# The down block product of a streaming encoder layer: accumulators first on VectorE, three plain feature pairs instead of two

## The chip, the cores and the metric

The kernel runs on one core of a Trainium2 chip. The metric is the device time of one execution in microseconds (us). One core has a matrix engine (TensorE, PE in the profile; PEld is its weight loading), VectorE (DVE), ScalarE (ACT), GpSimd (POOL) and SyncE (SP), which here only issues DMAs. TensorE accumulates in PSUM; everything else lies in SBUF or in DRAM.

## The reference

One inference step of an encoder layer for 1024 prompt frames and 32 sample frames, in fp32. The part that matters here is the feed-forward block, which stands before and after a token mixer (attention and gated linear attention, which the change doesn't touch):

```python
def swiglu(h, w_gate, w_up, w_down):
    return (jax.nn.silu(h @ w_gate) * (h @ w_up)) @ w_down

x = x + 0.5 * swiglu(rmsnorm(x, g_ffn1), w1g, w1u, w1d)     # FFN1
...                                                         # token mixer
x = x + 0.5 * swiglu(rmsnorm(x, g_ffn2), w2g, w2u, w2d)     # FFN2
x = rmsnorm(x, g_final)
```

The model width is 1024, the hidden width 2816, so `w_down` is 2816 x 1024. Prompt and sample frames share the weights and are treated as 1056 columns.

## The kernel before, in words

Activations are feature-major: `S.x` is eight tiles of 128 features x 1056 frames, the residual. A fp32 product is made of three fp32r products: each operand is split into a rounded high part (ACT, line 51) and the rest (DVE, line 55, or POOL, line 53), and hi·hi, hi·lo and lo·hi are summed in PSUM (`mm3`, lines 60 to 62).

Gate/up and down use one level of the Strassen-Winograd scheme: seven products of blocks for a 2 x 2 block product, in the order 1, 6, 7, 5, 2, 4, 3. Their right-hand sides are the hidden block B11, B21, B22 and the sums T1 to T4. The hidden features are 22 tiles of 128, in 11 pairs; one pair (256 features) is one gate and one up step. For the pairs 1 to 9 the gate/up stage computes the seven right-hand sides of the down product at once, splits them and stores them to DRAM (`keep`, lines 397 to 403: seven parts of 528 KB a pair). The pairs 0 and 10 are stored as plain hidden features (`hid_spill`, line 388 for pair 10; pair 0 is made elsewhere), since 11 is odd and the down stage multiplies two pairs at a time.

The down stage (class `Down`) walks over groups of pairs, `PAIRS = [(1, 2), (3, 4), (5, 6), (7, 8), (9,)]`, and in each group over m = 0..3, that is 256 of the 1024 output features: 20 steps (class `DownStep`). A step has seven products of 12 matmuls (128 x 264 columns), 84 in all; in the last group, which has one pair, 6 each, 42 in all. The seven products accumulate into four PSUM tiles (`pd_a` to `pd_d`, two banks each, one rotating pool of four): 1 and 2 into a, 6 into b, 7 and 4 into c, 5 and 3 into d. So product 3 can start only when what was read from d after product 5 has been read, and product 4 when c has been read after product 7.

What comes out of PSUM (`emit`, lines 498 to 539): `c1` = half of product 1 (ACT, line 523); `half` is one DVE instruction, 0.5·PSUM + y (line 505). It makes `u2` from b and c1, `u3` from c and u2, and adds a, c, d into the four half tiles of x that the step owns. POOL adds `u3` into x11 (line 530), `u2` into x10 (line 533) and `u2` into x01 (line 536). Before the change these POOL additions stand ahead of the DVE addition into the same x (for x11 in the same product's turn, for the others one or two products earlier), so the DVE instruction that reads d after product 5 needs POOL's line 530 done first.

A step's weights are loaded as one slab of 512 KB two steps ahead, and prepared one step ahead (`prep`, called after product 6): four POOL sums (lines 484 to 487), then splits into the weight tiles. Parts of the next group are loaded during a group into the 28 half-tile places of `S.h` and `S.X`. During the last group the hidden features of the plain pairs are loaded (line 630, halves of 264 KB, through the slab buffers) and split, and so are the plain slabs of `w_down`.

Then `plain` multiplies the four plain feature tiles: 3 chunks of 352 columns x 8 output tiles x 4 features x 3 matmuls = 288 matmuls; DVE adds each sum into x (line 654). What follows (a norm and the next projection, or the closing norm) starts out of `plain`.

The order of all instructions on an engine is set at build time by a scheduler that goes by priorities (roughly the order of the code) and models when operands are ready; at run time each engine runs its queue in order and waits on semaphores.

Of the kernel before, what the change touches and what calls it, by code (L numbers as in the profile page):

```python
# [8 lines left out]
F32 = mybir.dt.float32  # L9
# [6 lines left out]
P = 128  # L16
# [257 lines left out]
class Step:  # L274
# [89 lines left out]
    def out(self, q, u, ps):  # L364
# [12 lines left out]
        else:  # L377
# [4 lines left out]
            else:  # L382
                t = two(S.tmp.tile([P, HALF], F32, name="tc", tag="tc"))
                nc.vector.tensor_add(t, u, ps)  # L384
                nc.gpsimd.tensor_mul(two(hid), t, sg)  # L385
            if self.i == FT // 2 - 1:
                f, h = 2 + q // 2, q % 2
                nc.sync.dma_start(S.hidden[f][:, h * HALF : h * HALF + HALF], hid)
            elif q != 1:
                self.keep({0: "B11", 3: "B22", 2: "B21"}[q], hid)  # L390
            else:
                b11, b12, b21, b22 = (S.x[4 + n][:, :HALF] for n in range(4))
                for name, o, x, y in (("T1", b11, b12, b11), ("T3", b12, b22, b12), ("T2", b22, b22, b11), ("T4", b21, b21, b22)):
                    nc.vector.tensor_sub(o, x, y)  # L394
                    self.keep(name, o)
# [68 lines left out]

PAIRS = [(1, 2), (3, 4), (5, 6), (7, 8), (9,)]
PLAIN = (0, 1, 20, 21)


class DownStep:


    def __init__(self, D, g, m):
        self.D, self.S, self.g, self.m, self.n = D, D.S, g, m, len(PAIRS[g])
        self.odd = (4 * g + m) % 2

    def prep(self, raw):

        S, nc = self.S, self.S.nc
        w = self.n * P
        a = [raw[:, i * w : i * w + w] for i in range(4)]  # L480
        s12 = S.s32.tile([P, 512], F32, name="s12", tag="s1")[:, : 2 * w]
        s34 = S.s32.tile([P, 512], F32, name="s34", tag="s2")[:, : 2 * w]
        s1, s2, s3, s4 = s12[:, :w], s12[:, w:], s34[:, :w], s34[:, w:]
# [7 lines left out]
        ws = S.wp.tile([P, 2, 1024], F32R, name="whl", tag="w")  # L491
        split_to(S, wa[:, 0, : 2 * w], wa[:, 1, : 2 * w], raw[:, : 2 * w])
        split_to(S, ws[:, 0, : 2 * w], ws[:, 1, : 2 * w], s12)
        split_to(S, wb[:, 0, :w], wb[:, 1, :w], a[2])
        split_to(S, ws[:, 0, 2 * w : 4 * w], ws[:, 1, 2 * w : 4 * w], s34)
        cut = lambda t, i: t[:, :, i * w : i * w + w]
# [3 lines left out]
    def emit(self, between):  # L500
# [5 lines left out]
        for n, p in enumerate(ORDER):  # L506
# [5 lines left out]
            for s in range(2):  # L512
                for k in range(self.n):
                    b = self.D.part(self.g, n, k)
                    for i, (u, v) in enumerate(((0, 0), (0, 1), (1, 0))):
                        nc.tensor.matmul(  # L516
                            t[:, s, :SW], w[:, u, k * P : k * P + P], b[:, v, ss(s)],
                            start=fresh and k == 0 and i == 0, stop=k == self.n - 1 and i == 2, skip_group_check=not fresh,
                        )
            ps = t[:, :, :SW]  # L520
            if p == 1:
                c1 = new("s1")
                nc.scalar.activation(c1, ps, AF.Copy, scale=0.5)
            elif p == 6:
                u2 = new("u2", bufs=1)
                half(u2, ps, c1)
            elif p == 7:
                u3 = new("u3", bufs=1)
                half(u3, ps, u2)
                nc.gpsimd.tensor_add(x[1][1], x[1][1], u3)  # L530
            elif p == 5:
                half(x[1][1], ps, x[1][1])
                nc.gpsimd.tensor_add(x[1][0], x[1][0], u2)  # L533
            elif p == 2:
                half(x[0][0], ps, x[0][0])
                nc.gpsimd.tensor_add(x[0][1], x[0][1], u2)  # L536
            elif p == 4:
                half(x[1][0], ps, x[1][0])
            else:
                half(x[0][1], ps, x[0][1])  # L540
            between(n)


class Down:
# [3 lines left out]
    def __init__(self, S, wd):  # L548
# [7 lines left out]
            X[6:] + [h0(4), h0(5), h0(6), h0(7), h1(4), h1(5), h1(6), h1(7)],  # L556
        ]
        self.steps = [DownStep(self, g, m) for g in range(len(PAIRS)) for m in range(4)]
        self.raw = {}
# [14 lines left out]
    def load_step(self, i):  # L574

        if i >= len(self.steps):
            return
        st = self.steps[i]
        if st.n == 2 or st.m % 2 == 0:
            S = self.S  # L580
            self.raw[i] = self.load_w(*((S.raw, "wraw") if i % 4 < 2 else (S.raw2, "wraw2")))
            if st.n == 1:
                self.raw[i + 1] = self.raw[i][:, 512:]

# [19 lines left out]
    def strassen(self, xd):  # L604
# [4 lines left out]
        for i, st in enumerate(self.steps):  # L609

            def between(n):
                if n == 0:
                    self.load_step(i + 2)
                if n == 1:
                    self.prep(i + 1)
                if st.g < last and n % 2 == 0 and 4 * (n // 2) + st.m < 7:
                    self.load_part(st.g + 1, 4 * (n // 2) + st.m)
                if st.g == last and n in (1, 4):
                    self.plain_tile(st.m, n // 4)
                if st.g == last and n == 6:  # L620
                    self.plain_slab(st.m)

            st.emit(between)

    def plain_tile(self, i, h):

        S = self.S
        cols = slice(h * HALF, h * HALF + HALF)
        raw = S.raw.tile([P, 1024], F32, name="wraw", tag="wraw")[:, :HALF]
        S.nc.sync.dma_start(raw, S.hidden[i][:, cols])  # L630
        split_to(S, S.h[4 + i][:, 0, cols], S.h[4 + i][:, 1, cols], raw)

    def plain_slab(self, j):
        S = self.S
        r = self.load_w(S.raw2, "wraw2")
        if j == 3:
            w = S.wp.tile([P, 2, 1024], F32R, name="whl", tag="w")
            ws = [w[:, :, :512], w[:, :, 512:]]
        else:
            ws = [S.X[6 + 2 * j][:, :, :512], S.X[7 + 2 * j][:, :, :512]]  # L640
        for i in range(2):
            split_to(S, ws[i][:, 0], ws[i][:, 1], r[:, i * 512 : i * 512 + 512])
        self.ws = getattr(self, "ws", []) + [ws]
# [701 lines left out]
def body(tc, A):  # L1345
# [10 lines left out]
    with ExitStack() as top:  # L1356
# [35 lines left out]
        def ffn_pools(es, part, inner, between=None):  # L1392

            S.ps = opener(inner)("psf", 4, space=PSUM)
            parts = opener(part)("parts")
            S.X = [parts.tile([P, 2, HALF], F32R, name=f"part{k}") for k in range(12)]
            pool = opener(inner)
# [298 lines left out]
def layouts(i):  # L1696
# [4 lines left out]
    def down(w):  # L1701
        tile = lambda f, d: w[f * P : f * P + P, d * P : d * P + P]
        out = []
        for g in PAIRS:
# [4 lines left out]
            out += [np.concatenate(blocks[n : n + 8], 1) for n in range(0, len(blocks), 8)]  # L1709
        for m in range(4):  # L1710
            out.append(np.concatenate([w[f * P : f * P + P, m * 256 : m * 256 + 256] for f in PLAIN], 1))
        return c(np.stack(out))
# [57 lines left out]
```

## Time and profile before

| | us |
|---|---|
| runs | 2208.17 median of 3 (2199.53 to 2209.41) |
| the profiled execution's own time | 2208.22 |
| its span, first to last instruction | 2206.4 |
| down steps of FFN1: groups of two pairs | 492.01 to 669.09 |
| last group (pair 9) of FFN1 | 669.09 to 709.04 |
| plain products of FFN1 | 709.04 to about 760 |
| down steps of FFN2: groups of two pairs | 1927.26 to 2104.34 |
| last group of FFN2 | 2104.34 to 2144.16 |
| plain products of FFN2 | 2144.16 to about 2194.5 |
| closing norm | to 2206.4 |

A row of a timeline reads: start, duration, engine, line, operation, out<-in, shape, count, and in brackets the idle time of the engine before it and what released it. A row of the window table gives, for a stretch of the span, its length, then the busy time (and instructions) of PE, PEld, DVE, ACT and POOL, the granted TensorE clock as a share of full speed, the busy share of the DMA engines and GB/s. A row of waits gives who waited for whom, microseconds in total, how often and the longest. Matmuls are pipelined: a row's duration overlaps the next row's, so a rate is read from starts.

### The profile page before, as it was taken

The numbers are of one execution on the slowest core, as the hardware profiler recorded it, in microseconds if no ns is written. First come the engines' busy times: TensorE is split into PE (matmuls) and PEld (weight loads), VectorE is DVE, ScalarE is ACT, GpSimd is POOL, SyncE is SP. The second block draws the span as 40 slices with busy tenths as digits, with TensorE's granted clock in tenths as the row PEclk, the third lists the DMA queues.
The fourth block names the chain that finished last, engine by engine and source line by source line (L and its number), as shares of the span: only waits on it lengthen the run. The fifth ranks groups of instructions, "written<-read, shape, count | busy, mean of one in ns | idle before, by whom it ended". The sixth has DMA issues, their size and how long they took to land. (4 is left out here: it accounts for less than half of the span.)

```text
span 2206.4 us, 38879 instructions
## 1 busy us (share of the span) xinstructions
PE 2089.5 (95%) x15684; PEld 2011.2 (91%) x15684; DVE 1441.0 (65%) x2240; ACT 908.6 (41%) x1636; POOL 764.2 (35%) x665
## 2 busy tenths in 40 slices
PE   7999999999997999999999989899999999999978
PEld 6899999999997878888898987899999999999977
DVE  6866667655557756286676687686666676555566
ACT  6534334332223443345555556354333343322225
POOL 0143343346665221122223322101434433466640
PEclk9999999999998999999999999999999999999989
DMA  4134334379523300112203141231343343795322
GB/s 169 49 136 168 127 145 160 125 288 380 203 103 102 101 31 26 38 32 65 75 23 100 33 139 49 90 110 54 129 172 130 139 165 127 285 376 210 104 64 79
DMA packets 103316, 281.32 MB, mean 128 GB/s; under 512 B 10624, under 2 KB 31392, under 8 KB 103136
## 3 DMA queue, kind: packets, MB, share of 16 engines
q1 hardware_dynamic: 103136, 278.84, 35.7%
q8 instruction: 123, 2.02, 0.4%
q14 instruction: 57, 0.47, 0.1%
HBM read 179.87 MB, written 92.18 MB: 123 GB/s over the span
## 5 line engine op out<-in xcount | busy, mean ns | idle before, releaser
L335 PE MATMUL acc_a<-h,whl 128*128 128x264 f32 x1920 | 248.1, 285 | 2.0 <-DVE whl L55 2.0
L335 PE MATMUL acc_d<-part,S 128*128 128x264 f32 x1920 | 246.8, 284 | 0.0
L335 PEld LDWEIGHTS acc_a<-h,whl 128*128 128x128 f32 x1920 | 240.5, 190 | 2.2 <-DVE whl L55 2.2
L335 PEld LDWEIGHTS acc_d<-part,S 128*128 128x128 f32 x1920 | 238.7, 188 | 0.0
L60 PE MATMUL pj<-h,whl 128*128 128x352 f32 x576 | 206.8, 359 | 0.0
L61 PE MATMUL pj<-h,whl 128*128 128x352 f32 x576 | 194.2, 337 | 0.0
L62 PE MATMUL pj<-h,whl 128*128 128x352 f32 x576 | 193.4, 336 | 0.0
L51 ACT ACTIVATE x<-x 128x528 fp32r<-128x528 f32 x126 | 81.4, 646 | 203.9 <-DVE x L394 95.3
L51 ACT ACTIVATE S<-s 128x512 fp32r<-128x512 f32 x160 | 98.5, 627 | 161.3 <-PE acc_d L335 63.4
L319 POOL TENSOR_TENSOR s<-wraw,s 128x512 f32<-128x512 f32 x38 | 49.1, 1293 | 281.7 <-DVE S L55 281.7
L55 DVE TENSOR_TENSOR x<-x 128x528 fp32r<-128x528 f32 x126 | 96.0, 762 | 71.1 <-ACT x L51 68.5
L505 DVE SCALAR_TENSOR_TENSOR x<-pd_d,x 128x528 f32<-128x528 f32 x80 | 56.5, 706 | 131.1 <-POOL x L530 127.5
L385 POOL TENSOR_TENSOR x<-tc,x 128x528 f32<-128x528 f32 x60 | 103.5, 1725 | 110.7 <-DVE tc L384 103.7
L53 POOL TENSOR_TENSOR whl<-wraw,whl 128x1024 fp32r<-128x1024 f32 x28 | 69.6, 2486 | 170.9 <-ACT whl L51 170.7
L335 PE MATMUL acc_b<-h,S 128*128 128x264 f32 x960 | 124.6, 285 | 1.5 <-ACT h L51 1.2
L55 DVE TENSOR_TENSOR S<-s,S 128x512 fp32r<-128x512 f32 x160 | 123.5, 773 | 3.8 <-ACT S L51 2.5
L335 PE MATMUL acc_c<-part,S 128*128 128x264 f32 x960 | 124.2, 285 | 1.1 <-DVE hid L255 1.1
L335 PE MATMUL acc_c<-h,A 128*128 128x264 f32 x960 | 123.6, 285 | 0.0
L335 PEld LDWEIGHTS acc_b<-h,S 128*128 128x128 f32 x960 | 120.2, 188 | 1.9 <-ACT h L51 1.4
L335 PEld LDWEIGHTS acc_c<-part,S 128*128 128x128 f32 x960 | 119.6, 188 | 1.3 <-DVE hid L255 1.3
L335 PEld LDWEIGHTS acc_c<-h,A 128*128 128x128 f32 x960 | 119.7, 189 | 0.0
L306 POOL TENSOR_TENSOR s<-wraw 128x512 f32<-128x512 f32 x38 | 48.9, 1288 | 198.1 <-DVE S L55 198.1
(333 smaller groups left out, 5196.4 us busy)
## 6 DMA issues: line engine op xcount, KB each, us to landing
part_spill<-x SPq DMA_DIRECT2D x126, 528.0 KB, 2.8
h<-part_spill SPq DMA_DIRECT2D x72, 528.0 KB, 8.8
part<-part_spill SPq DMA_DIRECT2D x54, 528.0 KB, 9.2
wraw<-win SPq DMA_DIRECT2D x24, 512.0 KB, 3.4
wraw<-w1g SPq DMA_DIRECT2D x22, 512.0 KB, 3.5
wraw<-w1u SPq DMA_DIRECT2D x22, 512.0 KB, 3.4
wraw<-w1d SPq DMA_DIRECT2D x22, 512.0 KB, 4.3
wraw<-w2g SPq DMA_DIRECT2D x22, 512.0 KB, 3.6
```

What stands on the lines that cost most here:

```text
L51: nc.scalar.activation(hi, src, AF.Copy)
L53: nc.gpsimd.tensor_sub(lo, src, hi.bitcast(F32))
L55: nc.vector.tensor_sub(lo, src, hi.bitcast(F32))
L60: nc.tensor.matmul(out, w[:, 0, wsl], a[:, 0, asl], start=first, stop=False)
L61: nc.tensor.matmul(out, w[:, 0, wsl], a[:, 1, asl], start=False, stop=False)
L62: nc.tensor.matmul(out, w[:, 1, wsl], a[:, 0, asl], start=False, stop=last)
L306: eng.tensor_add(self.s1, a21, a22)
L319: eng.tensor_sub(src, a12, self.s2)
L335: nc.tensor.matmul(t[:, s, :SW], w[:, a, ks], m(k, b, s), start=fresh and k == 0 and n == 0, stop=k == 3 and n == 2, skip_group_check=not ...
L385: nc.gpsimd.tensor_mul(two(hid), t, sg)
L505: half = lambda out, ps, y: nc.vector.scalar_tensor_tensor(out, ps, 0.5, y, op0=ALU.mult, op1=ALU.add)
```

## The change

Four things change.

1. **Order of accumulation.** For the products 5, 4 and 3 the DVE instruction adds the PSUM tile into x first, and POOL adds u2 or u3 into the same half tile after it (line 534 of the new kernel). Sums are the same up to rounding.
2. **Buffers.** u2 goes to two tags in turn (by m), u3 into the two-buffer tag `tc`.
3. **Pairs.** Pair 9 leaves the block product: the group of four half steps is gone, and `plain` multiplies six features (0, 1, 18 to 21): 432 matmuls instead of 288. In gate/up pair 9 is stored as plain hidden features, as pair 10 was, without sums, splits and parts.
4. **Places.** The twelve half tiles `S.X` become halves of six whole tiles `S.XX`. The plain features lie in `S.h[0..3]` and `S.XX[0..1]`; their twelve halves are loaded through the second slab pool during the last group's four steps (three a step). The six plain slabs go into `S.XX[2..5]` and two weight buffers: two are issued in the last two steps, four at the start of `plain`.

The diff, cut to its core:

```diff
@@ gate/up, after a product
-            if self.i == FT // 2 - 1:
-                f, h = 2 + q // 2, q % 2
-                nc.sync.dma_start(S.hidden[f][:, h * HALF : h * HALF + HALF], hid)
+            f, h = 2 * self.i + q // 2, q % 2
+            if f in PLAIN:
+                nc.sync.dma_start(S.hidden[PLAIN.index(f)][:, h * HALF : h * HALF + HALF], hid)
             elif q != 1:
                 self.keep({0: "B11", 3: "B22", 2: "B21"}[q], hid)
...
-PAIRS = [(1, 2), (3, 4), (5, 6), (7, 8), (9,)]
-PLAIN = (0, 1, 20, 21)
+PAIRS = [(1, 2), (3, 4), (5, 6), (7, 8)]
+PLAIN = (0, 1, 18, 19, 20, 21)
...
@@ DownStep.emit
             elif p == 6:
-                u2 = new("u2", bufs=1)
+                u2 = new(f"u{2 + self.odd}", bufs=1)
                 half(u2, ps, c1)
             elif p == 7:
-                u3 = new("u3", bufs=1)
+                u3 = new("tc")
                 half(u3, ps, u2)
-                nc.gpsimd.tensor_add(x[1][1], x[1][1], u3)
-            elif p == 5:
-                half(x[1][1], ps, x[1][1])
-                nc.gpsimd.tensor_add(x[1][0], x[1][0], u2)
-            elif p == 2:
-                half(x[0][0], ps, x[0][0])
-                nc.gpsimd.tensor_add(x[0][1], x[0][1], u2)
-            elif p == 4:
-                half(x[1][0], ps, x[1][0])
             else:
-                half(x[0][1], ps, x[0][1])
+                r, h, u = {5: (1, 1, u3), 2: (0, 0, None), 4: (1, 0, u2), 3: (0, 1, u2)}[p]
+                half(x[r][h], ps, x[r][h])
+                if u is not None:
+                    nc.gpsimd.tensor_add(x[r][h], x[r][h], u)
...
@@ Down.strassen
-                if st.g == last and n in (1, 4):
-                    self.plain_tile(st.m, n // 4)
-                if st.g == last and n == 6:
-                    self.plain_slab(st.m)
+                if st.g == last and n % 2 == 0 and n < 6:
+                    self.plain_tile(3 * st.m + n // 2)
+                if st.g == last and n == 5 and st.m > 1:
+                    self.plain_slab()
...
+    def plain_tile(self, n):
+        S = self.S
+        cols = slice(n % 2 * HALF, n % 2 * HALF + HALF)
+        raw = S.raw2.tile([P, 1024], F32, name="wraw2", tag="wraw2")[:, :HALF]
+        S.nc.sync.dma_start(raw, S.hidden[n // 2][:, cols])
+        t = self.tiles[n // 2]
+        split_to(S, t[:, 0, cols], t[:, 1, cols], raw)
+
+    def plain_slab(self):
         S = self.S
+        r = self.load_w(S.raw, "wraw")
+        j = len(self.ws)
+        w = S.wp.tile([P, 2, 1024], F32R, name="whl", tag="w") if j in (1, 5) else S.XX[2 + j - (j > 1)][:, :, :1024]
+        split_to(S, w[:, 0], w[:, 1], r)
+        self.ws.append(w)
...
@@ Down.plain
+        n = len(PLAIN)
+        while len(self.ws) < 6:
+            self.plain_slab()
         for c in range(NCH):
             for d in range(KT):
                 pd = S.ps.tile([P, CW], F32, name="pd", tag="acc")
-                for i in range(4):
-                    o = (i % 2) * 256 + (d % 2) * P
-                    mm3(nc, pd, self.ws[d // 2][i // 2], slice(o, o + P), S.h[4 + i], cs(c), i == 0, i == 3)
+                for i in range(n):
+                    b = d // 2 * n + i
+                    o = b % 4 * 256 + d % 2 * P
+                    mm3(nc, pd, self.ws[b // 4], slice(o, o + P), self.tiles[i], cs(c), i == 0, i == n - 1)
```

The scheduler moves instructions. POOL's queue in a regular step of FFN1 (a group of two pairs) of the kernel before; `s12`, `s34` are the weight sums, `x_76` the residual, `u2`, `u3` the partial sums:

```order
L484 TENSOR_TENSOR s12_6470<-wraw_6329 128x256
L485 TENSOR_TENSOR s12_6470<-s12_6470,wraw_6329 128x256
L486 TENSOR_TENSOR s34_6471<-wraw_6329 128x256
L487 TENSOR_TENSOR s34_6471<-wraw_6329,s12_6470 128x256
L533 TENSOR_TENSOR x_76<-x_76,u2_6346 128x528
L536 TENSOR_TENSOR x_76<-x_76,u2_6346 128x528
L530 TENSOR_TENSOR x_76<-x_76,u3_6378 128x528
```

And of the changed kernel (`tc` holds u3):

```order
L484 TENSOR_TENSOR s12_6321<-wraw_6178 128x256
L485 TENSOR_TENSOR s12_6321<-s12_6321,wraw_6178 128x256
L486 TENSOR_TENSOR s34_6322<-wraw_6178 128x256
L487 TENSOR_TENSOR s34_6322<-wraw_6178,s12_6321 128x256
L534 TENSOR_TENSOR x_76<-x_76,tc_6227 128x528
L534 TENSOR_TENSOR x_76<-x_76,u2_6195 128x528 x2
```

The same seven instructions stand in one place; the addition of u3, which was last, is now the first of the three, and each has moved from ahead of the DVE instruction on the same half tile to behind it.

VectorE's queue at the end of the last down step of FFN1 and the start of `plain`, in the kernel before; `h7` is a plain feature tile, `pd_*` the PSUM tiles:

```order
L505 SCALAR_TENSOR_TENSOR u2_7703<-pd_b_7696,s1_7694 128x528
L55 TENSOR_TENSOR h7_91<-wraw_7705,h7_91 128x528
L505 SCALAR_TENSOR_TENSOR u3_7716<-pd_c_7709,u2_7703 128x528
L505 SCALAR_TENSOR_TENSOR x_76<-pd_a_7687,x_76 128x528
L505 SCALAR_TENSOR_TENSOR x_76<-pd_d_7719,x_76 128x528
L55 TENSOR_TENSOR h7_91<-wraw_7736,h7_91 128x528
L505 SCALAR_TENSOR_TENSOR x_76<-pd_c_7709,x_76 128x528
L505 SCALAR_TENSOR_TENSOR x_76<-pd_d_7719,x_76 128x528
L55 TENSOR_TENSOR whl_7756<-wraw2_7754,whl_7756 128x512 x2
```

And in the changed kernel, at the same place (`part0`, `part1` are now plain feature tiles, `part2` to `part5` and `whl` hold plain slabs, `tc` is u3; the step's a is row 8, its c row 9):

```order
L55 TENSOR_TENSOR part1_105<-wraw2_7350,part1_105 128x528
L55 TENSOR_TENSOR whl_7402<-wraw_7400,whl_7402 128x1024
L505 SCALAR_TENSOR_TENSOR u3_7333<-pd_b_7320,s1_7314 128x528
L55 TENSOR_TENSOR part1_105<-wraw2_7382,part1_105 128x528
L55 TENSOR_TENSOR part3_107<-wraw_7435,part3_107 128x1024
L505 SCALAR_TENSOR_TENSOR tc_7348<-pd_c_7335,u3_7333 128x528
L505 SCALAR_TENSOR_TENSOR x_76<-pd_d_7354,x_76 128x528
L55 TENSOR_TENSOR part4_108<-wraw_7439,part4_108 128x1024
L505 SCALAR_TENSOR_TENSOR x_76<-pd_a_7301,x_76 128x528
L505 SCALAR_TENSOR_TENSOR x_76<-pd_c_7335,x_76 128x528
L55 TENSOR_TENSOR part5_109<-wraw_7443,part5_109 128x1024
```

The last split of a feature tile and the split of a plain slab now stand ahead of `tc`, and another slab's split stands ahead of the reading of a and c at the end of the step.

More of the change, by code (lines that the diff above doesn't have):

```diff
@@ L458, in gate_up @@
                 tail(p)
[L465 to L466 removed]
+PAIRS = [(1, 2), (3, 4), (5, 6), (7, 8)]
+PLAIN = (0, 1, 18, 19, 20, 21)
 class DownStep:
     def __init__(self, D, g, m):
[L473 to L474 removed]
+        self.D, self.S, self.g, self.m = D, D.S, g, m
+        self.odd = m % 2
     def prep(self, raw):
         S, nc = self.S, self.S.nc
[L479 removed]
+        w = 2 * P
         a = [raw[:, i * w : i * w + w] for i in range(4)]
[L481 to L482 removed]
+        s12 = S.s32.tile([P, 512], F32, name="s12", tag="s1")
+        s34 = S.s32.tile([P, 512], F32, name="s34", tag="s2")
         s1, s2, s3, s4 = s12[:, :w], s12[:, w:], s34[:, :w], s34[:, w:]
@@ L512, in emit @@
             for s in range(2):
-                for k in range(self.n):
+                for k in range(2):
                     b = self.D.part(self.g, n, k)
@@ L517, in emit @@
                             t[:, s, :SW], w[:, u, k * P : k * P + P], b[:, v, ss(s)],
-                            start=fresh and k == 0 and i == 0, stop=k == self.n - 1 and i == 2, skip_group_check=not fresh,
+                            start=fresh and k == 0 and i == 0, stop=k == 1 and i == 2, skip_group_check=not fresh,
                         )
@@ L557, in __init__ @@
         ]
+        self.tiles = S.h[:4] + S.XX[:2]
+        self.ws = []
         self.steps = [DownStep(self, g, m) for g in range(len(PAIRS)) for m in range(4)]
@@ L574, in load_step @@
     def load_step(self, i):
[L576 to L583, printed above, removed]
+        if i < len(self.steps):
+            self.raw[i] = self.load_w(*((self.S.raw, "wraw") if i % 4 < 2 else (self.S.raw2, "wraw2")))
     def prep(self, i):
@@ L1395, in ffn_pools @@
             parts = opener(part)("parts")
-            S.X = [parts.tile([P, 2, HALF], F32R, name=f"part{k}") for k in range(12)]
+            S.XX = [parts.tile([P, 2, NR], F32R, name=f"part{k}") for k in range(6)]
+            S.X = [S.XX[k // 2][:, :, k % 2 * HALF : k % 2 * HALF + HALF] for k in range(12)]
             pool = opener(inner)
@@ L1709, in down @@
             out += [np.concatenate(blocks[n : n + 8], 1) for n in range(0, len(blocks), 8)]
-        for m in range(4):
-            out.append(np.concatenate([w[f * P : f * P + P, m * 256 : m * 256 + 256] for f in PLAIN], 1))
+        blocks = [w[f * P : f * P + P, m * 256 : m * 256 + 256] for m in range(4) for f in PLAIN]
+        out += [np.concatenate(blocks[n : n + 4], 1) for n in range(0, len(blocks), 4)]
         return c(np.stack(out))
@@ L1749 @@
     A["xs"] = nc.dram_tensor("x_spill", (KT, P, NR), F32, kind="Internal").ap()
-    A["hid"] = nc.dram_tensor("hid_spill", (4, P, NR), F32, kind="Internal").ap()
-    A["parts"] = nc.dram_tensor("part_spill", (FT // 2 - 2, 7, P, 2, HALF), F32, kind="Internal").ap()
+    A["hid"] = nc.dram_tensor("hid_spill", (len(PLAIN), P, NR), F32, kind="Internal").ap()
+    A["parts"] = nc.dram_tensor("part_spill", (FT // 2 - 3, 7, P, 2, HALF), F32, kind="Internal").ap()
     A["os"] = nc.dram_tensor("o_spill", (2, P, NR), F32, kind="Internal").ap()
```

21 lines of the change are left out of this document (3 added, 18 removed).

## The prediction

> **What bounds the kernel now.** I read the page's engine totals and slices first.
>
> ```profile
> PE 2089.5 (95%) x15684; PEld 2011.2 (91%) x15684; DVE 1441.0 (65%) x2240; ACT 908.6 (41%) x1636; POOL 764.2 (35%) x665
> PE   7999999999997999999999989899999999999978
> PEclk9999999999998999999999999999999999999989
> ```
>
> TensorE is busy for 95% of the span; its weak slices lie at the start, at the end of each feed-forward block (slice 13 ends at 717 us, the dip near the end at 2151) and in the mixer. So a change of the down stage gains where TensorE idles there, and it pays for each matmul that it adds. I cut the down stages into steps, last group and plain products, in a table of windows (length, busy PE, PEld, DVE, ACT, POOL, clock, DMA share, GB/s).
>
> ```profile
> 492.01:502.24 10.23, 10.23 (x87) 10.23 (x86) 4.45 (x7) 1.66 (x3) 5.84 (x5) 1.00 0.98 369
> 492.01:669.09 177.08, 166.97 (x1346) 164.40 (x1345) 96.95 (x159) 45.54 (x83) 110.04 (x110) 1.00 0.61 227
> 669.09:709.04 39.95, 27.15 (x170) 24.63 (x169) 29.63 (x48) 11.89 (x25) 21.17 (x23) 0.88 0.29 91
> 1927.26:2104.34 177.08, 166.92 (x1347) 164.33 (x1346) 96.94 (x159) 45.56 (x83) 110.07 (x110) 1.00 0.61 225
> 2104.34:2144.16 39.82, 27.14 (x170) 24.41 (x168) 30.12 (x50) 12.33 (x25) 21.05 (x20) 0.86 0.24 75
> 2144.16:2194.70 50.54, 50.49 (x292) 49.78 (x292) 32.34 (x68) 26.95 (x51) 0.00 (x0) 0.94 0.17 58
> 709.00:713.00 4.00, 4.00 (x16) 4.00 (x15) 3.72 (x3) 1.06 (x1) 2.40 (x1) 0.50 0.46 147
> 2144.00:2150.50 6.50, 6.34 (x23) 6.34 (x24) 2.18 (x5) 1.09 (x2) 0.00 (x0) 0.53 0.00 0
> ```
>
> The first step waits for nothing and takes 10.23 us. Sixteen of them would take 163.7, the stage takes 177.08: 13.4 us of waits in each block. The last group of half steps holds 27.15 us of matmuls in 39.95. Plain products start at half the clock in both blocks. Who makes PE wait in the full steps (waits in that window: total, times, longest), and one period of it in the timelines of POOL, DVE and PE:
>
> ```profile
> DVE x L505 <- POOL x L530: 54.9, 16, 3.9
> PE pd_d L516 <- DVE x L505: 10.1, 12, 1.0
> ```
>
> ```profile
> 581.60 1.07 POOL L484 TENSOR_TENSOR s<-wraw 128x256 f32<-128x256 f32 x1 [4.25 <-issue]
> 584.83 1.33 POOL L533 TENSOR_TENSOR x<-x,u 128x528 f32<-128x528 f32 x1
> 586.12 1.33 POOL L536 TENSOR_TENSOR x<-x,u 128x528 f32<-128x528 f32 x1
> 587.39 1.32 POOL L530 TENSOR_TENSOR x<-x,u 128x528 f32<-128x528 f32 x1
> 588.75 0.71 DVE L505 SCALAR_TENSOR_TENSOR x<-pd_d,x 128x528 f32<-128x528 f32 x1 [3.77 <-POOL x L530]
> 592.97 1.06 POOL L484 TENSOR_TENSOR s<-wraw 128x256 f32<-128x256 f32 x1 [4.25 <-issue]
> 512.03 1.74 PE L516 MATMUL pd_d<-part,whl 128*128 128x264 f32 x12 [0.87 <-DVE x L505]
> ```
>
> It is a ring. POOL prepares weights (581.60), adds u2, u2 and u3 (to 588.71); only then may DVE read d after product 5 (588.75), and PE's product 3 writes into d after that. The next weights' sums start at 592.97, 11.37 us after the last. POOL is busy for about 7.1 us of it (581.60 to 588.71) and idle for 4.25: it is the order, not a full engine, that makes a period of 11.37 out of 10.23.
>
> **The change part by part.** *Accumulators first, two buffers.* DVE's reading of d after product 5 no longer needs POOL. POOL's three additions come after it and are wanted only when the step's half tiles of x are touched again, a group (four steps) later, and when u2 or u3's buffer comes round, two steps later. The cost is at most nothing new: POOL has the same seven instructions.
>
> ```profile
> L505 DVE SCALAR_TENSOR_TENSOR x<-pd_d,x 128x528 f32<-128x528 f32 x31 | 21.9, 705 | 55.6 <-POOL x L530 54.9 <-PE pd_d L516 0.6
> L55 DVE TENSOR_TENSOR whl<-s,whl 128x512 fp32r<-128x512 f32 x28 | 18.2, 686 | 0.1
> ```
>
> Next in line is DVE's chain u2, u3, d: product 5's result is read within about 0.7 us once it is there, and product 3 starts two products (2 x 1.46 us) later, so 2 us are spare. I take 10.23 us a step. Gain per block 13.4 us; the bounds are 10.1 (what PE idled) and 13.4. Two blocks: **-26.8**.
>
> *The group of half steps goes.* All of both windows: **-79.8** (39.95 + 39.82).
>
> *144 more plain matmuls a block.* Their rate, from the timeline of PE:
>
> ```profile
> 709.04 0.50 PE L60 MATMUL pd<-h,part 128*128 128x352 f32 x1
> 713.13 0.32 PE L62 MATMUL pd<-h,part 128*128 128x352 f32 x1
> 715.23 0.33 PE L60 MATMUL pd<-h,part 128*128 128x352 f32 x1
> 718.13 0.32 PE L60 MATMUL pd<-h,part 128*128 128x352 f32 x1
> ```
>
> From 715.23 to 718.13 eighteen matmuls start, 0.161 us each: 144 of them are 23.2 us, both blocks **+46.4**. Their DVE additions into x stay as many, with more time between.
>
> *The slow start of plain.* The first 14 matmuls took 4.09 us, 0.293 each at a clock of 0.50: 1.85 us lost in FFN1; in FFN2 the 23 matmuls of a window of 6.50 us at 0.53 would take 3.7, 2.8 lost. It followed waits in the half steps:
>
> ```profile
> 703.75 1.00 PE L516 MATMUL pd_c<-part,A 128*128 128x264 f32 x6 [2.06 <-DVE u L505]
> 707.55 1.69 PE L516 MATMUL pd_d<-part,whl 128*128 128x264 f32 x6 [2.81 <-DVE x L505]
> ```
>
> With full steps in front I count it as gone, **-4.7**; the bound on the other side is that it stays, 0. [...]
>
> *Gate/up's step of pair 9* loses four DVE sums, seven splits and seven stores of 528 KB, and gains two stores. The two gate/up stages, as windows:
>
> ```profile
> 76.00:491.00 415.00, 410.37 (x3351) 409.55 (x3351) 273.08 (x353) 160.57 (x255) 166.96 (x116) 1.00 0.42 154
> 1488.00:1926.00 438.00, 438.00 (x3599) 438.00 (x3599) 284.28 (x374) 171.11 (x270) 165.45 (x116) 1.00 0.40 147
> ```
>
> PE idles for 4.6 us in 415 and for none in 438, so I cost it at **0**: matmuls hide that work, and only the group that is gone waited for the parts of pair 9. The bounds are a gain of 4.6 us and, if those two stores hold up the loads behind them in SP's queue by one load of 2.7 us, a loss of that.
>
> *Loads at the end of the down stage.* Here the change can cost. Twelve feature halves must pass two slab buffers, which hold the weights of the last steps, and each needs a load, a split on ACT and one on DVE; two slabs are split ahead of the end too.
>
> ```profile
> wraw<-hid_spill SPq DMA_DIRECT2D x7, 264.0 KB, 2.7
> wraw<-w1d SPq DMA_DIRECT2D x2, 512.0 KB, 3.9
> h<-part_spill SPq DMA_DIRECT2D x72, 528.0 KB, 8.8
> L51 ACT ACTIVATE h<-wraw 128x528 fp32r<-128x528 f32 x16 | 10.2, 639 | 14.7 <-DMA wraw<-hid_spill 9.2 <-PE pd_d L516 5.5
> L55 DVE TENSOR_TENSOR h<-wraw,h 128x528 fp32r<-128x528 f32 x16 | 12.2, 765 | 0.0
> L55 DVE TENSOR_TENSOR whl<-wraw,whl 128x1024 fp32r<-128x1024 f32 x48 | 76.3, 1590 | 28.1 <-ACT whl L51 28.1
> ```
>
> A link is 2.7 + 0.64 + 0.77 and some 0.2 for the issue, 4.3 us. Counting from the start of the group's first step, the fourth half can be issued at about 10 us (one buffer free, the other holds the last step's slab); three links of 4.3 go through one buffer, six more at 2.15 through two: the last half is split at 10 + 12.9 + 12.9 + 1.4 = 37.2 us. The last step starts at 3 x 10.23 = 30.7; its product 4 is due at 30.7 + 5 x 1.46 = 38.0 and needs `tc`, which stands in DVE's queue behind that half's split and a slab's (1.59) and takes 0.7: 39.5, so PE waits 1.5 us. The first plain matmul needs the reading of c after product 4, which stands behind another slab's split, loaded (3.9) only when an earlier slab's buffer is free: another 1.5. That makes 3 us a block; I add half again for a stretch of half clock and for splits that meet POOL: 4.5, both blocks **+9**. The bounds are 0 (loads a little faster than that) and about 15 us a block (nine links, each held up by one POOL addition of 1.33, and the 3 us).
>
> That splits meet POOL shows here:
>
> ```profile
> 692.43 1.49 POOL L536 TENSOR_TENSOR x<-x,u 128x528 f32<-128x528 f32 x1
> 692.67 1.53 DVE L55 TENSOR_TENSOR whl<-s,whl 128x256 fp32r<-128x256 f32 x1
> 694.33 0.41 DVE L55 TENSOR_TENSOR whl<-s,whl 128x256 fp32r<-128x256 f32 x1
> ```
>
> The same split took 1.53 us beside a POOL addition and 0.41 alone. The Trainium skill ("SBUF — State Buffer", "Who interferes with whom") has it that a VectorE instruction with two SBUF inputs and a GpSimd one that reads SBUF exclude each other, and that one with a single SBUF input is free of it; the rows agree for the split, and L505, which reads PSUM and one tile, keeps its 0.71 us beside POOL.
>
> The sum on the profiled execution's own time, 2208.22 (the median is 2208.17, so nothing is to be moved between them): -26.8 - 79.8 + 46.4 - 4.7 + 9 = -55.9, **2152 us**. The closing norm, about 12 us after the last plain matmul, stays.
>
> **The rivals.** *No new wait at the end* (0.2). The last half is split 1.5 us too late by my count, after links of 4.3 us; links that are 0.3 us shorter (6 x 0.3 = 1.8 by the last half) take the wait at `tc` away, and the other one shrinks with it. Then 2152 - 9 = 2143. For it: DMA is busy for 0.29 of the last group, so loads run alone. Against it: `tc` is queued behind a split whose data cannot be there before 35 us.
>
> *VectorE and GpSimd hold each other up* (0.15). In a regular step POOL works for 3.2 us on sums (581.60 to 584.83) and 3 x 1.33 on x, 7.2, and DVE for at most 4 x 0.69 = 2.8 on splits: 10.0 of 10.23 if they exclude each other. In the last group three feature halves (3 x 0.77) come on top, 12.3 a step: 2.1 over in three steps, 6 us a block, 12 in both, if no queue is ahead: 2164. If the regular steps lose their gain to it (26.8) and the last group does not, 2179. Against it: DVE shows 3.77 us idle in each period, and weights are a step ahead.
>
> *The feature halves come late* (slower; 0.04). Their price is nine links, three whole and six shared by two buffers. If a load takes as long as the parts do (8.8 us instead of 2.7), a link grows by 6.1, the last half by 3 x 6.1 + 6 x 3.05 = 36.6 us, in both blocks 73: 2225. It ends as slow as before from 4.7 us more a link (12 x 4.7 = 56). For it: the parts' 8.8 us. Against it: those ran while DMA was 0.61 to 0.98 busy; halves in the last group took 2.7.
>
> *The gain is taken back elsewhere* (0.04): PE's plain matmuls wait for slabs four to six, whose loads are issued at the start of plain only. They would have to be late by 28 us a block to come to 2208; three loads one after the other with their splits take 3 x (3.9 + 1.05 + 1.59) = 19.6, of which 8.7 lie under the first three output tiles (54 matmuls).
>
> **How the numbers follow.** The forecast, with waits of 2 to 8 us a block at the end of the last step, has 0.57; its own range is 2146 to 2161. No new wait 0.2, engines in each other's way 0.15, late halves 0.04, taken back 0.04. The range 2138 to 2174 takes in the second and most of the third; its lower end is 5 us under 2143, since the runs of before lie up to 9 us apart. By 0.5% (11 us, what a measurement of this kernel can tell from none) it is faster with 0.92 (the first three cases), the same with 0.04, slower with 0.04.
>
> **What would show it right or wrong.** Right: DVE's L505 has no wait on POOL in the full steps, which follow each other at 10.23 us and take 164 us a block; plain has 432 matmuls in 70 us at 0.161 each, with a clock near 1 from the start; PE's idle at the end of the last step is 2 to 8 us, released by DVE. Wrong: steps at 11.3 us (then POOL is the bound after all); the first plain matmul later than 175 us after the first step (late halves); PE idle inside plain behind a split of a slab; gate/up longer than 415 and 438 us.

## The result, and the profile after

The changed kernel takes **2152.84 us** (median of 4 runs, 2149.15 to 2154.39) against 2207.46 (4 runs, 2199.53 to 2209.41): ratio 0.9757, 95% interval 0.973 to 0.9784. The forecast was 2152, in a range of 2138 to 2174. Measured again beside three of the experiments it took 2153.87 (0.9757, 0.9743 to 0.9771).

The stages of the profiled executions, from the starts of the first matmuls of each:

| us | before | after | difference | forecast |
|---|---|---|---|---|
| start to FFN1's down steps | 492.01 | 494.93 | +2.9 | 0 |
| down steps of FFN1 | 217.03 | 171.30 | -45.7 | -48.8 |
| plain products of FFN1, to the mixer's first matmul | 51.39 | 71.02 | +19.6 | +21.3 |
| mixer and gate/up of FFN2 | 1166.83 | 1155.67 | -11.2 | 0 |
| down steps of FFN2 | 216.90 | 171.30 | -45.6 | -48.7 |
| plain products of FFN2 and closing norm | 62.24 | 83.18 | +20.9 | +20.4 |
| span | 2206.4 | 2147.4 | -59.0 | -55.9 |

(Forecast of the steps: 16 x 10.23 and 4.5 of waits instead of 217.03 and 216.90; of plain: 23.2 less the slow start.) The down and plain stages differ by 50.8 us. The first and the fourth row hold gate/up too, which the change touches, but the difference doesn't lie there: from line 335's first matmul behind the mixer to the first down step it took 409.08 us before and 409.71 after. The rest of the fourth row is the mixer, and belongs to noise as far as the runs tell: the changed kernel, profiled once more, took 1162.05 us for this row instead of 1155.67, and one program (run e6 below) 1160.03 in one execution and 1167.23 in another.

Engine totals and clock of the page, and windows of the trace after (length, busy PE, PEld, DVE, ACT, POOL, clock, DMA share, GB/s):

```profile
PE 2069.2 (96%) x15636; PEld 1998.0 (93%) x15636; DVE 1442.3 (67%) x2142; ACT 892.2 (42%) x1586; POOL 742.8 (35%) x609
PEclk9999999999999999999999999999999999999999
```

```profile
494.93:666.23 171.30, 165.35 (x1347) 164.08 (x1345) 133.38 (x169) 52.14 (x89) 115.88 (x103) 1.00 0.65 232
666.23:737.25 71.02, 71.02 (x436) 70.59 (x437) 43.92 (x77) 24.29 (x46) 15.10 (x11) 1.00 0.26 88
1892.92:2064.22 171.30, 165.53 (x1347) 164.19 (x1345) 132.49 (x168) 51.99 (x89) 115.73 (x100) 1.00 0.64 230
2064.22:2135.40 71.18, 71.18 (x436) 70.55 (x436) 35.60 (x70) 29.07 (x53) 3.53 (x2) 1.00 0.14 49
```

The plain products run without a gap, at full clock from their start. What is odd is DVE: in the 16 full steps of FFN1 it was busy for 96.95 us before and for 133.38 now. Some 16 of these 36 us are splits of plain features and slabs, which lie in these steps now. The groups of the other splits and of POOL's additions in this stage say where most of the rest comes from (busy us, mean ns | idle before); the first row is POOL's addition of u2 before, the others are after:

```profile
L533 POOL TENSOR_TENSOR x<-x,u 128x528 f32<-128x528 f32 x16 | 21.2, 1325 | 11.8 <-DVE u L505 11.8
L55 DVE TENSOR_TENSOR whl<-s,whl 128x512 fp32r<-128x512 f32 x28 | 33.8, 1240 | 3.6 <-ACT whl L51 3.4
L505 DVE SCALAR_TENSOR_TENSOR x<-pd_d,x 128x528 f32<-128x528 f32 x31 | 21.8, 703 | 10.4 <-PE pd_d L516 10.4
L534 POOL TENSOR_TENSOR x<-x,u 128x528 f32<-128x528 f32 x30 | 48.4, 1621 | 22.7 <-DVE x L505 22.5
```

The ring is gone: what line 505 waits for at d is PE, no longer POOL. The split of a weight sum took 686 ns on average and now takes 1240; POOL's addition of u2 took 1.32 us and now takes 1.62; line 505, with one operand in PSUM, stays at 0.70. Before, the ring made POOL's additions and DVE's splits take turns. Now they run at the same time and hold each other up. The Trainium skill ("SBUF — State Buffer", "Who interferes with whom") says that a VectorE instruction with two SBUF inputs and a GpSimd one that reads SBUF exclude each other and that one with a single SBUF input is free of it: the rows agree.

All of PE's waits in FFN1's down stage, from its timeline (start, duration, ..., idle before <- releaser):

```profile
533.95 1.73 PE L516 MATMUL pd_c<-part,A 128*128 128x264 f32 x12 [0.85 <-DVE tc L505]
617.96 1.74 PE L516 MATMUL pd_d<-part,whl 128*128 128x264 f32 x12 [0.34 <-DVE x L505]
628.66 1.73 PE L516 MATMUL pd_c<-h,S 128*128 128x264 f32 x12 [1.66 <-DVE tc L505]
649.67 1.73 PE L516 MATMUL pd_c<-h,S 128*128 128x264 f32 x12 [0.23 <-DVE tc L505]
661.89 1.71 PE L516 MATMUL pd_c<-h,A 128*128 128x264 f32 x12 [1.71 <-DVE tc L505]
666.23 0.43 PE L60 MATMUL pd<-h,part 128*128 128x352 f32 x1 [1.16 <-DVE x L505]
```

The last two are those that the prediction priced at 1.5 us each, at the places it named. The first four, 3.1 us, it did not have. All but 1.2 us of the six lie in the last group and at its end, where VectorE splits the plain features and slabs too. They don't all have one cause. Ahead of the first wait, ACT's split of a weight sum, and DVE's behind it, wait for the sum itself, which stands behind u2's addition in POOL's queue:

```profile
529.04 0.63 ACT L51 ACTIVATE whl<-s 128x512 fp32r<-128x512 f32 x1 [4.26 <-POOL s L485]
529.71 0.69 DVE L55 TENSOR_TENSOR whl<-s,whl 128x512 fp32r<-128x512 f32 x1 [1.99 <-ACT whl L51]
```

DVE's and POOL's timelines ahead of the third and longest of the four show three splits in a row, each stretched, between DVE and `tc`:

```profile
620.72 1.83 DVE L55 TENSOR_TENSOR h<-wraw,h 128x528 fp32r<-128x528 f32 x1
623.10 2.40 DVE L55 TENSOR_TENSOR whl<-s,whl 128x512 fp32r<-128x512 f32 x2
625.42 1.76 DVE L55 TENSOR_TENSOR part<-wraw,part 128x1024 fp32r<-128x1024 f32 x1
627.90 0.71 DVE L505 SCALAR_TENSOR_TENSOR tc<-pd_c,u 128x528 f32<-128x528 f32 x1
```

```profile
623.25 1.70 POOL L534 TENSOR_TENSOR x<-x,u 128x528 f32<-128x528 f32 x1 [1.26 <-DVE x L505]
624.90 1.19 POOL L484 TENSOR_TENSOR s<-wraw 128x256 f32<-128x256 f32 x1
626.18 1.59 POOL L485 TENSOR_TENSOR s<-s,wraw 128x256 f32<-128x256 f32 x1
```

### The profile page after: what moved, and what is told of

Read it like the earlier page. It is cut to its first block, busy times and chain, and to the rows that moved or that the text cites. A ratio compares the mean times of both kernels' runs of the same rounds, so it can differ in the third digit from the quotient of the medians.

```text
span 2147.4 us, 38446 instructions
## 1 busy us (share of the span) xinstructions
PE 2069.2 (96%) x15636; PEld 1998.0 (93%) x15636; DVE 1442.3 (67%) x2142; ACT 892.2 (42%) x1586; POOL 742.8 (35%) x609
## 4 chain that ended last, share of the span: by engine, by line
PE 77%; DVE 13%; ACT 3%; issue 3%; DMA 2%; POOL 1%; DVEq 0%; SPq 0%; ACTq 0%; POOLq 0%
PE acc_a L335 11%; PE acc_c L335 11%; PE acc_d L335 11%; PE acc_b L335 5%; PE acc L243 4%; PE pj L60 3%; PE pj L61 3%; PE pj L62 3%; PE pd_c L516 3%; PE pd_a L516 2%; PE pd_d L516 2%; DVE f L1206 2%; PE pd L60 2%; PE pd L62 2%; PE pd L61 2%
## 5 line engine op out<-in xcount | busy, mean ns | idle before, releaser
L60 PE MATMUL pj<-h,whl 128*128 128x352 f32 x576 | 203.9, 354 | 0.0
L61 PE MATMUL pj<-h,whl 128*128 128x352 f32 x576 | 191.1, 332 | 0.0
L62 PE MATMUL pj<-h,whl 128*128 128x352 f32 x576 | 190.8, 331 | 0.0
L51 ACT ACTIVATE x<-x 128x528 fp32r<-128x528 f32 x112 | 72.4, 647 | 180.8 <-DVE x L394 84.8
L55 DVE TENSOR_TENSOR x<-x 128x528 fp32r<-128x528 f32 x112 | 85.3, 761 | 63.1 <-ACT x L51 60.8
L534 POOL TENSOR_TENSOR x<-x,u 128x528 f32<-128x528 f32 x64 | 103.5, 1624 | 49.5 <-DVE x L505 49.0
```

The lines of the kernel that those rows point to most:

```text
L51: nc.scalar.activation(hi, src, AF.Copy)
L55: nc.vector.tensor_sub(lo, src, hi.bitcast(F32))
L60: nc.tensor.matmul(out, w[:, 0, wsl], a[:, 0, asl], start=first, stop=False)
L61: nc.tensor.matmul(out, w[:, 0, wsl], a[:, 1, asl], start=False, stop=False)
L62: nc.tensor.matmul(out, w[:, 1, wsl], a[:, 0, asl], start=False, stop=last)
L534: nc.gpsimd.tensor_add(x[r][h], x[r][h], u)
```

## The experiments

The theory: the order of accumulation opens the ring (13 us a block), the group of half steps was limited by VectorE and POOL and not by its matmuls, and what is left is waiting behind DVE's queue at the end. The rivals: the second buffers did it; the third plain pair is a loss; what is left is VectorE and GpSimd excluding each other. Each run stands beside runs of the kernel before on the same chip.

### One part of the change alone

*The order and buffers, five groups and two plain pairs* (e1):

```diff
 # kernel before, DownStep.emit as in the change; PAIRS and PLAIN stay
-                nc.gpsimd.tensor_add(x[1][1], x[1][1], u3)     # ahead of half(), by product
+                half(x[r][h], ps, x[r][h])
+                if u is not None:
+                    nc.gpsimd.tensor_add(x[r][h], x[r][h], u)
```

> The new order of accumulation and the two buffers alone; five groups and two plain pairs as before. Theory: the order takes the waits out of the full steps (16 steps 177.1 -> 164 to 167 us a block) and the slow start out of plain, but the four half steps then are bound by VectorE, which was busy for 29.6 us there, and take about 30 instead of 39.9: about 2208 - 2 x (12 + 10) - 4 = 2160 us (2154 to 2166), slower than the whole change (2153). Rival: the half steps come down to their matmuls too (4 x 42 x 0.122 = 20.5 us): then about 2140, and the third plain pair (23.2 us of matmuls for 20.5) would be a loss.

Measured: 2169.12 against 2205.74, ratio 0.9832 (0.9811 to 0.9853). Its full steps and its half steps in FFN1, as windows:

```profile
491.97:656.80 164.83, 163.97 (x1347) 163.75 (x1346) 121.92 (x161) 45.60 (x84) 119.55 (x108) 1.00 0.66 244
656.80:691.50 34.70, 25.81 (x171) 23.59 (x169) 33.24 (x47) 12.46 (x26) 21.27 (x23) 0.90 0.30 95
```

The 16 full steps come down from 177.08 to 164.83, as forecast; the half steps only to 34.70, with DVE busy for 33.24 of it. So the time of that group is DVE's, more than the 30 I expected, and the rival (20.5) is out. The whole time lies above the 2154 to 2166 expected. Before, DVE was busy for 29.63 us in this group with about as many instructions, which fits that POOL holds it up here, too. In the full steps the splits are as long as in the changed kernel, and yet PE waits only once there, 0.86 us:

```profile
L55 DVE TENSOR_TENSOR whl<-s,whl 128x512 fp32r<-128x512 f32 x28 | 33.3, 1225 | 3.6 <-ACT whl L51 3.4
```

So longer splits cost little by themselves where VectorE has room. In the changed kernel most of PE's waits come in the last group, where VectorE has the features and slabs on top.

*Three plain pairs, order and buffers of before* (e2):

```diff
 # changed kernel, with emit of before
-                half(x[r][h], ps, x[r][h])
-                if u is not None:
-                    nc.gpsimd.tensor_add(x[r][h], x[r][h], u)
+                nc.gpsimd.tensor_add(x[1][1], x[1][1], u3)     # and so on, as in the kernel before
```

> Three plain pairs and four groups, with the order of accumulation and the single buffers of before. Theory: the ring of POOL and DVE stays, 16 steps take about 177 us a block and those of the last group some more (the tile splits lie in the ring): about 2153 + 2 x 9 = 2171 us (2165 to 2180), VectorE's line 505 waiting for POOL again. Rival, that the order has no part in the gain: 2153.

Measured: 2184.06, ratio 0.9898 (0.9873 to 0.9922); slower than expected. Two of PE's rows of a regular step and of the last group:

```profile
569.54 1.73 PE L516 MATMUL pd_d<-h,whl 128*128 128x264 f32 x12 [0.87 <-DVE x L505]
639.99 2.13 PE L516 MATMUL pd_d<-h,whl 128*128 128x264 f32 x12 [2.30 <-DVE x L505]
```

The ring stays, 0.87 us a step, and with the features' splits in it the last group's steps wait for up to 2.30: the down stage takes 187.36 us in FFN1, where I had taken about 180, and 185.84 in FFN2. In FFN1 the granted clock fell, too:

```profile
625.00:682.20 57.20, 48.81 (x354) 47.42 (x353) 39.48 (x55) 19.36 (x31) 25.70 (x24) 0.91 0.31 96
```

By an estimate from this row (0.09 of 48.81 us of matmuls, or of all 57.2) that is 4 to 5 of the 7 us. The order (with its buffers) alone is worth 36.6 us, the pairs alone 21.7, both together 54.6 in the first comparison. The sum of the two is 58.3; with the intervals of these runs that can't be told from 54.6.

*One buffer each for u2 and u3* (e5):

```diff
-                u2 = new(f"u{2 + self.odd}", bufs=1)
+                u2 = new("u2", bufs=1)
-                u3 = new("tc")
+                u3 = new("u3", bufs=1)
```

> The changed kernel with one buffer each for u2 and u3, the order as changed. Theory: what made the ring was the order; with one buffer VectorE's u2 waits for POOL's last addition of the step before, which ends about 1.6 us ahead of it in the regular steps: 0 to 0.5 us a step, 2153 to 2165, I take 2157. Rival, that the buffers are what breaks the ring: steps at 11.1 to 11.4 us again, 2179 or more.

Measured: 2154.79 (2151.91 to 2158.03), ratio 0.9767 (0.9744 to 0.979). That is the changed kernel's time within what can be told, and the down stages take 171.81 and 171.05 us, where the changed kernel's take 171.30 each. The order opens the ring; the second buffers have no measurable part in it. Two buffers with the old order were not run.

### What the waits that are left come from

*Without POOL's additions* (e4; x lacks u2 and u3, so the output is another one):

```diff
-                if u is not None:
-                    nc.gpsimd.tensor_add(x[r][h], x[r][h], u)
```

> The changed kernel without POOL's three additions of u2 and u3 into x (the output lacks them): POOL only makes the weight sums. It prices what VectorE and GpSimd cost each other. If the waits that are left in the down steps (5.9 us of PE idle a block) come from VectorE and GpSimd excluding each other: splits of 128x512 fall from 1.24 us back to 0.69, the 16 steps go from 171.3 to about 165 us a block, 2153 - 12 = 2141. If they come from late loads of the plain features in VectorE's queue: splits fall all the same, but 169 to 171 us stay, 2149 to 2153. I expect something between, 2146.

Measured: 2139.57, ratio 0.9697 (0.9677 to 0.9718), below the 2146 expected and close to the first theory's 2141. The split's group and PE's only two waits in FFN1:

```profile
L55 DVE TENSOR_TENSOR whl<-s,whl 128x512 fp32r<-128x512 f32 x28 | 18.2, 688 | 0.1
```

```profile
654.10 1.74 PE L516 MATMUL pd_c<-h,A 128*128 128x264 f32 x12 [0.44 <-DVE tc L505]
657.87 0.43 PE L60 MATMUL pd<-h,part 128*128 128x352 f32 x1 [0.58 <-DVE x L505]
```

The split is back at 688 ns; the down stage takes 165.33 and 164.27 us, and FFN2 has no wait in it at all. So POOL's additions cost 13 us of the 2153, though no instruction of PE or DVE waits for their result. This run takes away both what they do: they lengthen the splits, and they stand ahead of the weight sums in POOL's queue (DVE's idle time before these splits falls from 3.6 to 0.1 us). It doesn't divide the 13 us between the two.

*The plain features earlier* (e3): twelve halves in three steps of the last group instead of four, half of them through the slab pool that is free there.

```diff
+EARLY = [(0, 2), (0, 4), (0, 6), (1, 1), (1, 3), (1, 4), (1, 5), (1, 6), (2, 1), (2, 2), (2, 3), (2, 5)]   # (m, n)
-                if st.g == last and n % 2 == 0 and n < 6:
-                    self.plain_tile(3 * st.m + n // 2)
+                if at in EARLY:
+                    k = EARLY.index(at)
+                    self.plain_tile(k, k in (0, 1, 2, 3, 4, 6))      # these through S.raw
```

> The changed kernel with the plain features loaded earlier: the twelve halves in the first three steps of the last group, the first six through the slab pool that is free there, and the two slabs half a step later and earlier. If the waits at the end (1.71 and 1.16 us in FFN1) come from late loads in VectorE's queue, they go, and some of the 2.0 us at the group's start with them: 3 us a block less, 2147 (2144 to 2150). If what counts is that VectorE's splits and GpSimd's additions exclude each other, the same splits in three steps instead of four only move the waits into these: 2151 to 2155.

Measured: 2153.43, beside 2153.87 for the changed kernel (ratios 0.9755 and 0.9757). PE's waits in FFN1's last group with what follows them, and its first plain matmul in FFN2:

```profile
633.23 1.72 PE L517 MATMUL pd_d<-h,whl 128*128 128x264 f32 x12 [0.91 <-DVE x L506]
638.16 2.54 PE L517 MATMUL pd_c<-h,A 128*128 128x264 f32 x12 [1.74 <-DVE tc L506]
640.49 2.39 PE L517 MATMUL pd_d<-h,whl 128*128 128x264 f32 x12
642.72 1.62 PE L517 MATMUL pd_a<-part,S 128*128 128x264 f32 x12
```

```profile
638.00:640.00 2.00, 1.84 (x10) 1.84 (x11) 0.80 (x3) 0.76 (x2) 1.83 (x2) 0.69 0.29 98
640.00:642.00 2.00, 2.00 (x11) 2.00 (x10) 2.00 (x4) 0.82 (x2) 0.11 (x1) 0.50 0.15 17
```

```profile
2068.69 0.32 PE L60 MATMUL pd<-h,part 128*128 128x352 f32 x1
```

The waits at the end are gone, and a wait of the same length stands two steps earlier. The time is that of the second expectation, but its reason holds in part only: PE's waits in the down stages fell, from 6.0 to 3.5 us in FFN1 and from 5.8 to 4.1 in FFN2. In their place came a stretch of slow clock behind two waits about 5 us apart (0.69 and 0.50 in the windows above; 0.76 and 0.50 in FFN2), where two products of 12 matmuls took 4.56 us, against 1.46 each elsewhere: 1.6 us in each block. The changed kernel has 1.00 in these steps. So the loads do set how much PE waits; the gain was lost again to the clock, and the down stages take 170.56 and 170.77 us instead of 171.30.

*The three additions on VectorE* (e6), the same sums:

```diff
-                    nc.gpsimd.tensor_add(x[r][h], x[r][h], u)
+                    nc.vector.tensor_add(x[r][h], x[r][h], u)
```

> The changed kernel with the three additions of u2 and u3 on VectorE, right behind the accumulator's. If mutual exclusion of VectorE and GpSimd makes the waits that are left, there is less of it (GpSimd reads for 3.2 us a step instead of 7.2), and VectorE has 4.3 (seven readings of PSUM) + 2.1 (splits) + 1.9 (additions) = 8.3 of 10.23 us to do: regular steps without waits, the last group (three more splits, 10.2) with a few: 2148 (2143 to 2153). If VectorE's own queue is what is late, three more instructions in it make it later: steps of 10.5 us and more in the last group, 2158 or more.

Measured: **2143.2**, ratio 0.9709 (0.9695 to 0.9722), and once more 2144.14 (0.972, 0.9698 to 0.9742): 10 us less than the change, the fastest kernel of this study that computes the reference. The groups of splits and additions, and PE's waits in FFN1:

```profile
L55 DVE TENSOR_TENSOR whl<-s,whl 128x512 fp32r<-128x512 f32 x28 | 25.1, 896 | 0.5 <-ACT whl L51 0.5
L534 DVE TENSOR_TENSOR x<-x,u 128x528 f32<-128x528 f32 x30 | 21.5, 716 | 0.0
```

```profile
624.76 1.75 PE L516 MATMUL pd_c<-h,S 128*128 128x264 f32 x12 [1.39 <-DVE tc L505]
659.70 0.43 PE L60 MATMUL pd<-h,part 128*128 128x352 f32 x1 [0.96 <-DVE x L505]
```

DVE has 48 instructions more in this stage (46 in the trace) and PE waits less for it: 2.4 us instead of 6.0. An addition takes 0.72 us there instead of 1.3 to 1.6 on POOL, and the splits meet only the weight sums.

*Early features, and only u3's addition on VectorE* (e7):

```diff
-                    nc.gpsimd.tensor_add(x[r][h], x[r][h], u)
+                    (nc.vector if p == 5 else nc.gpsimd).tensor_add(x[r][h], x[r][h], u)
```

> The early loads, and one of the three additions (u3 into x11) on VectorE, two on GpSimd: between the two above if both help, 2145 (2141 to 2150); 2151 to 2156 if neither does.

Measured: 2152.73 (2147.14 to 2154.19), ratio 0.9747 (0.9731 to 0.9762): no gain to be told. Its splits:

```profile
L55 DVE TENSOR_TENSOR whl<-s,whl 128x512 fp32r<-128x512 f32 x28 | 35.0, 1286 | 2.1 <-ACT whl L51 2.0
```

They take as long as in the changed kernel (1240) and with the early loads alone (1181). u3's addition comes early in a step, beside DVE's readings of PSUM; the two additions of u2 come at a step's end, beside the splits, and it seems to be these that stretch them (to move u2's alone was not tried). POOL's queue was shorter by one addition a step here, and nothing was won; but DVE had that addition to do, so this says little about the queue.

### Around the best version

*Additions on VectorE and early features* (e9):

```diff
 # e3, with
-                    nc.gpsimd.tensor_add(x[r][h], x[r][h], u)
+                    nc.vector.tensor_add(x[r][h], x[r][h], u)
```

> The three additions on VectorE and the early loads of the plain features together. What is left of PE's waits in the down steps is 2.4 us a block in FFN1 and 1.1 in FFN2, half of it at the end of the last step. If these are late loads, both blocks gain 1 to 2 us: 2141. If VectorE is full in the last group's first three steps (four tile splits a step instead of three: 8.3 + 2.5 = 10.8 of 10.23 us), they grow there: 2143 to 2147, which I expect after the run with the early loads alone.

Measured: 2143.89, ratio 0.9717 (0.9695 to 0.9738), beside 2144.14 for e6: no difference, and within the 2143 to 2147 expected.

*Additions on VectorE, but five groups and two plain pairs* (e10):

```diff
 # e1, with
-                    nc.gpsimd.tensor_add(x[r][h], x[r][h], u)
+                    nc.vector.tensor_add(x[r][h], x[r][h], u)
```

> The new order with the three additions on VectorE, but five groups and two plain pairs. It tells whether the third plain pair is worth its place when VectorE and GpSimd no longer hold each other up. By the matmuls the half steps (20.5 us) are cheaper than the pair in plain (23.2): 2143 - 5 = 2138. By VectorE's work a half step holds 7 readings (4.3), 3 additions (1.9), splits of the weights (1.2), a tile (1.2) and half of a slab: about 9 us for 5.1 of matmuls, 36 for the group: 2143 + 2 x (36 - 23) = 2169. I expect 2160 (2153 to 2170).

Measured: 2164.48, ratio 0.9811 (0.9787 to 0.9834). Full steps and half steps of FFN1:

```profile
492.64:656.35 163.71, 163.71 (x1347) 163.71 (x1345) 137.31 (x207) 45.64 (x84) 52.79 (x62) 1.00 0.66 245
656.35:689.18 32.83, 24.81 (x170) 22.74 (x168) 32.49 (x59) 12.51 (x26) 4.98 (x11) 0.92 0.31 103
```

Here the sixteen steps take 163.71 us without any wait, 10.23 each, which is the bound that the prediction used. The time is within the 2153 to 2170 expected. And the half steps take 32.83 with DVE busy for 32.49 of them: the pair costs 20.5 us of matmuls there and 23.2 in plain, but DVE's share of a step does not halve with its matmuls. The third plain pair is worth 20 us (2164.5 against 2144.1) with additions on VectorE and 15 to 16 (2169.1 against 2152.8 to 2153.9) with additions on POOL.

*Low halves of the plain features on GpSimd* (e11):

```diff
 # e6, and in plain_tile
-        split_to(S, t[:, 0, cols], t[:, 1, cols], raw)
+        split_to(S, t[:, 0, cols], t[:, 1, cols], raw, True)     # the second part on POOL
```

> The three additions on VectorE, and the low halves of the plain features made by GpSimd, which is idle for 7 us a step now. If VectorE's load is what is left, 12 instructions less in the last group: 1 to 2 us a block, 2141. If exclusion decides, GpSimd's 1.3 us for each tile block VectorE's splits as its additions did: 2145 to 2149. I expect the second, since that is what the twelve additions of the last group did.

Measured: 2157.77, ratio 0.9779 (0.976 to 0.9799), 14 us worse than e6, and worse than either expectation. DVE in the last group, and ACT just before:

```profile
618.39 1.35 DVE L55 TENSOR_TENSOR A<-wraw,A 128x256 fp32r<-128x256 f32 x1 [2.59 <-ACT A L51]
```

```profile
617.40 0.65 ACT L51 ACTIVATE h<-wraw 128x528 fp32r<-128x528 f32 x1 [3.65 <-DMA wraw<-hid_spill]
617.95 0.40 ACT L51 ACTIVATE A<-wraw 128x256 fp32r<-128x256 f32 x1
```

DVE waits here for a weight's split on ACT, which stands in ACT's queue behind a feature half whose load was not there yet. So not only exclusion (1.35 us for a split of 0.41) is at work: the queues came out in another order, too. And with waits of up to 2.29 us in the last group of FFN1 the clock falls:

```profile
617.00:665.88 48.88, 43.63 (x326) 42.77 (x326) 40.06 (x52) 18.71 (x30) 21.76 (x21) 0.93 0.34 106
```

By an estimate from this row (0.07 of 43.63 us of matmuls, or of all 48.88) the clock takes about 3 of the 6.5 us that this down stage is longer than e6's (173.15 against 166.69). The down stages of the two blocks, 6.5 and 7.2 us longer than e6's, make up all of the 14 us. How the rest divides between exclusion and the order of the queues was not tried.

## Why the prediction was right, point by point

- **The ring, -26.8.** Right in cause and nearly in size. The order and the buffers alone took the full steps of FFN1 from 177.08 to 164.83 us (e1), 12.3 of the 13.4 forecast; with one buffer the gain is the same (e5), so of "the order and two buffers" it is the order that is needed.
- **"The cost is at most nothing new: POOL has the same seven instructions."** This step failed. The instructions are the same but now meet DVE's splits, and at times stand ahead of the next weight sums: 13 us of the 2153 (e4), 10 of which can be had back (e6). In the sum it shows as 171.30 us of down steps where 168.2 were forecast, 3.1 us a block. The rival on VectorE and GpSimd had the mechanism and the place: the regular steps lost little, the last group most. It added 6 us a block to the forecast, about twice what came.
- **The half steps, -79.8, and the matmuls for them, +46.4.** Right: plain grew by 19.6 and 20.9 us, where 23.2 less the slow start gives 21.3 and 20.4. FFN1's row grew by a little less, since before it held a wait of 1.77 us of the following norm (748.15); after, the nearest such wait, 0.78 us, comes behind the mixer's first matmul (742.04, 737.25) and so outside the row.
- **The slow start, -4.7.** Right: plain starts at full clock, after waits of 1.71 and 1.16 us, where before waits of 2.06 and 2.81 us came ahead of 4.09 us at 0.50. "With full steps in front" is not enough as a reason, though: in e3 the clock fell to 0.50 among full steps, behind waits of 0.91 and 1.74 us.
- **New waits at the end, +9.** Right in place and in size for FFN1 (1.71 and 1.16 against 1.5 and 1.5), less in FFN2 (1.25 and 0.52, together just under the 2 to 8 us named as a sign). Their cause was taken for late loads with some stretching by POOL, and both have a part: with earlier loads the waits at the end go (e3), and without POOL's additions 0.44 and 0.58 us of them stay in FFN1 and none in FFN2 (e4). But e3 took no time off the whole, so faster loads alone would hardly have made the rival "no new wait" come true.
- **Gate/up, 0.** Right: 409.08 us before and 409.71 after in FFN2. The step of pair 9 gained four stores of 264 KB, not two; that cost nothing to be seen.
- **The sum.** -55.9 was forecast; the down and plain stages gave -50.8, the medians -54.6. The 5 us between are the down steps' 3.1 a block, less 1 in plain; and about 4 came back outside these stages, where executions of one program differ by 7. That 2152 met 2152.84 so closely is in part luck: a miss of 5 us and noise of 4 went opposite ways.

## What to carry to other kernels

When an engine waits for another one's work that it doesn't need yet, turning the order round opens the ring without taking work away; a second buffer isn't always part of it. But two engines that took turns will then run side by side, and may make each other's instructions longer: compare the mean of the same group before and after, not only the waits. Look at the granted clock beside the waits: a change that saves waiting can lose it again there. And a part that halves TensorE's work but not the vector engine's is not cheaper, however few matmuls it has.

## What the runs showed that I had not expected

- VectorE's splits nearly doubled, from 686 to 1240 ns, beside the additions that GpSimd now did at the same time, and went back to 688 without these. In regular steps this hardly cost anything (e1); in the last group it did. Doing the same additions on VectorE, the busier of the two engines, made the kernel 10 us faster.
- Moving one of three additions (e7, with the early loads) gave nothing and moving all three gave 10 us. Which of them overlaps the splits seems to decide.
- Giving 12 splits in each last group to GpSimd, which was idle for about 7 us a step (e11), cost 14 us.
- Two waits of 0.91 and 1.74 us, about 5 us apart, were followed by a clock of 0.50 (e3), while waits of 1.71 and 1.16 us, 4.3 us apart, left it at 1.00 in the changed kernel. What separates the two was not tried.
